# A two-layer hybrid decoder step in float32: sums of weights by adding DMAs, and modulation units spread over the blocks

## The chip, the core and the metric

The kernel runs on one core of a Trainium2 chip. Its time is the device time of one execution in microseconds. Before the change it is 3188.43 us, the median of three runs (3184.79 to 3195.4).

TensorE multiplies, VectorE and ScalarE work on vectors, GpSimd adds and multiplies and issues DMAs of its own queue, SyncE issues the loads. The profile calls them PE (PEld for its loads of weights), DVE, ACT, POOL and SP. Each takes its instructions in the order in which they were written and waits on semaphores for the others.

## The reference, cut to what matters

```python
for l in range(2):
    ada = silu(c) @ w_ada + b_ada                      # 9 vectors: shift, scale, gate of three parts
    h = rms(x) * g_ffn1 * (1 + sc1) + sh1
    x = x + 0.5 * gt1 * ((silu(h @ w1_a) * (h @ w3_a)) @ w2_a)
    h = rms(x) * g_mix * (1 + sc2) + sh2
    x = x + gt2 * mixer(h)                             # retention, conv module, short conv
    h = rms(x) * g_ffn2 * (1 + sc3) + sh3
    x = x + 0.5 * gt3 * ((silu(h @ w1_b) * (h @ w3_b)) @ w2_b)
y = rms(x) * g_final
```

There are 512 prompt positions and 8 sequences of 8 sample positions, 576 tokens in all. The model width is 1024, the SwiGLU width is 2816, everything is float32.

## The kernel before, in words

Activations lie transposed, 128 features by 576 tokens, in two halves of 288 tokens. Each float32 factor is split into a high part, which is a copy rounded to `float32r`, and a low part, which is what the rounding lost. A product is three matmuls: high by high, high by low, low by high. The high part of a weight tile is made by ScalarE (`nc.scalar.copy`, L195 and L209), the low part by VectorE (the subtraction of `rest`, L131).

**The SwiGLUs.** There are four: a and b of layer 0, then a and b of layer 1. Each has 22 column tiles `f` of `w1` and `w3`. From f = 4 on, two tiles f and f + 1 are taken together in a *seven-product block* (`seven`, L544): with quarters of `h` and of the two weight tiles, seven products of 128x512 by 512x288 give what eight would. The sums of `h` that this needs are made once (`forms`). The sums of weights are made for each block (`sums`, L213). If `a` is the raw tile of f and `b` that of f + 1, and 1 and 2 are their halves, the block needs X = a, Y with b1 + a1 in the first half of b, S = b1 + b2, and Z = a with S added to its first half and that sum of first halves to its second. GpSimd makes S, Y and Z with four additions of 128x512, in place in the raw tiles and in the buffer `s1`, of which there is one. X, S, Y and Z are each split into high and low (`halves`).

TensorE's products in a block come in the order X0, Y0, X1, Z0, S, Y1, Z1, twelve matmuls each. The first three are copied or combined on ScalarE and VectorE in between: X0's product is copied to `s1` of that function (L572), `u` is that copy plus Y0's product (L576), and Z0 adds to the bank from which `u` was made, so it waits for L576. X1 adds to the bank that L572 reads.

A SwiGLU has 18 blocks, for `w1` and `w3` by turns, in four runs of 2, 6, 4 and 6. After each run come eight *down steps*, products with `w2` over the tiles so far (the last run ends the SwiGLU).

**What sets the order.** Every engine's program is written out in the order of the Python calls. `pump` (L138), called between products, issues the loads that come next, as long as fewer than four raw tiles are held, and takes at most one *job* a call from the list that `sums` made: X's split, the additions for Z, then the splits of S, Y and Z. There are five buffers of high and low parts, so S waits until X is free, Y for S, and Z for Y. With the splits of Y and Z a raw tile each is given back, and `pump` issues the load into it (L166); SP, in its turn, waits until the old contents have been read.

**Modulation.** The vectors `ada` are a product of 9 columns with `w_ada`, cut into units (`ada_unit`, L339) of two tiles of 128x512, loaded by SP (L135) and multiplied in eight small matmuls (L349). All units run in layer 0: 56 fill its first SwiGLU and 72 its second, two after each block or pair of tiles and one after each down step, two after each down step where there are 72. Of their tiles, fewer than four are loaded ahead once the first SwiGLU is under way, and a tile counts as free three calls of `pump` after its unit.

Of the kernel before, what the change touches and what calls it, by code (L numbers as in the profile page):

```python
# [24 lines left out]
ALU = mybir.AluOpType  # L25
# [44 lines left out]
class Trunk:  # L70
# [142 lines left out]
    def sums(self, key, a, b):  # L213

        add = self.nc.gpsimd.tensor_add
        s = self.wp.tile([128, 512], F32, tag="s1", bufs=1, name=self.name("s1"))
        add(s, b[:, :512], b[:, 512:])
        add(b[:, :512], b[:, :512], a[:, :512])  # L220

        def z():
            self.rest()
            add(a[:, :512], a[:, :512], s)
            add(a[:, 512:], a[:, 512:], a[:, :512])

        def zh():
            self.halves((*key, "Z"), a)
            self.held -= 1

        def yh():
            self.halves((*key, "Y"), b)
            self.held -= 1

        self.jobs.extend(((1, lambda: self.halves((*key, "X"), a)), (0, z),
                          (1, lambda: self.halves((*key, "S"), s, 512)), (1, yh), (1, zh)))

    def part(self, key, which):
# [8 lines left out]
    def free(self, key):  # L247
        if key[0] == "ada":
            if self.quota > 8:
                self.gone.append(self.calls + 3)  # L250
            else:
                self.whole -= 1
        elif key not in self.spare:
            self.live -= 1
        del self.split[key]
# [285 lines left out]
            self.nc.vector.tensor_sub(lo, z[:, HB:], hi.bitcast(F32))  # L541
        self.zs = None

    def seven(self, key, post):  # L544

        nc = self.nc
        mm = nc.tensor.matmul
        h = [(x[0][:, :NT], x[1]) for x in self.h]
        quarter = lambda k, j: [(x[0][:, j * HB:(j + 1) * HB], x[1][:, j * HB:(j + 1) * HB]) for x in h[4 * k:4 * k + 4]]

        def product(ps, which, at, xs, first, last):
            hi, lo = self.part(key, which)
            for i, x in enumerate(xs):
                c = slice(512 * at + 128 * i, 512 * at + 128 * i + 128)
                k = dict(skip_group_check=True)
                mm(ps, hi[:, c], x[0], start=first and i == 0, stop=False, **k)  # L556
                mm(ps, hi[:, c], x[1], start=False, stop=False, **k)  # L557
                mm(ps, lo[:, c], x[0], start=False, stop=last and i == 3, **k)  # L558

        bank = lambda: self.lin(HB)  # L560
        free = lambda which: self.free((*key, which))
        def more():
            self.rest()
            for fn in self.after:
                fn()
            self.after = []
            self.pump(True)

        p, q = bank(), bank()
        product(p, "X", 0, quarter(0, 0), True, True)  # L570
        s1 = self.temp([128, HB])
        nc.scalar.copy(s1, p)  # L572
        more()
        product(q, "Y", 0, self.T[7], True, True)
        u, v = self.temp([128, HB]), s1
        nc.vector.tensor_add(u, s1, q)  # L576
        more()
        product(p, "X", 1, quarter(1, 0), False, True)
        free("X")
        post(0, 0, p)  # L580
        more()
        self.ada_done()
        product(q, "Z", 0, self.T[2], False, True)
        nc.vector.tensor_sub(v, s1, q)
        nc.vector.tensor_sub(u, u, q)
        more()
        r = bank()
        product(r, "S", 0, self.T[5], True, True)
        free("S")
        post(1, 1, v, r)  # L590
        more()
        t = bank()
        product(t, "Y", 1, self.T[4], True, True)
        free("Y")
        post(1, 0, v, t)
        more()
        product(r, "Z", 1, quarter(1, 1), False, True)
        free("Z")
        post(0, 1, u, r)
        self.rest()  # L600
        self.pump(True, False)
# [175 lines left out]
    def ffn(self, l, ab, sh, fill, first, last):  # L777

        w1, w3, w2 = "w1" + ab, "w3" + ab, "w2" + ab
        fill = deque(fill)  # L780
# [13 lines left out]
        def add_fill(n):  # L794
            for _ in range(min(n, len(fill))):
                u = fill.popleft()
                self.steps.append(([("ada", *u, i) for i in range(2)], lambda u=u: self.ada_unit(*u)))

        pairs = [[(w1, l, f), (w3, l, f)] for f in range(FT)]
# [30 lines left out]
        def one_pair(f):  # L830
            if f == 1:
                forms = self.forms()
                go(forms, 2)
                self.bg.append(forms)
            pair_step(pairs[f])

        acts = {}

        def duo_step(f, up):
            nc = self.nc  # L840
            if up == 0:
                for i in range(2):
                    g[f + i] = (self.slot([128, NT], F32R, "ghi"), self.slot([128, NT], F32R, "glo"))

            def up1(i, j, a, b=None):
                t = self.temp([128, HB])
                if b is None:
                    nc.scalar.activation(t, a, AF.Silu)
                else:
                    if i == 0:  # L850
                        nc.vector.tensor_add(t, a, b)
                    else:
                        nc.vector.scalar_tensor_tensor(t, a, -1.0, b, ALU.mult, ALU.subtract)
                    nc.scalar.activation(t, t, AF.Silu)
                acts[i, j] = t

            def up3(i, j, a, b=None):
                s = acts.pop((i, j))
                if b is None:
                    nc.vector.tensor_mul(s, s, a)  # L860
                else:
                    t = self.temp([128, HB])
                    if i == 0:
                        nc.vector.tensor_add(t, a, b)
                    else:
                        nc.vector.scalar_tensor_tensor(t, a, -1.0, b, ALU.mult, ALU.subtract)
                    nc.gpsimd.tensor_mul(s, s, t)  # L867
                c = slice(j * HB, (j + 1) * HB)
                hi, lo = (x[:, c] for x in g[f + i])

                def halves():
                    nc.scalar.copy(hi, s)
                    nc.vector.tensor_sub(lo, s, hi.bitcast(F32))  # L873

                waiting.append(halves)

            waiting = []

            def late(i, j, a, b=None):
                before = list(waiting)  # L880
                waiting.clear()
                up3(i, j, a, b)
                for fn in before:
                    fn()

            self.seven(pairs[f][up], late if up else up1)
            self.after += waiting
            if f + 2 in [at for at, _ in GROUPS] + [FT]:
                for fn in self.after:
                    fn()  # L890
                self.after = []
            if up and f + 2 == FT:
                self.T = None
# [18 lines left out]
        nfill = len(fill)  # L912
        for gi, (f0, n) in enumerate(GROUPS):
            for f in range(f0, f0 + n):
                if f == 0:
                    ks = [("ada", 0, 1, k, i) for k in range(8) for i in range(2)]
                    ks = [("do", "more_x")] + pairs[0] + ks if first else pairs[0] + pairs[1]
                    self.steps.append((ks, opening))
                elif f > 3:
                    for up in range(2 - f % 2 * 2):  # L920
                        ks = [pairs[f][up], pairs[f + 1][up]]
                        self.steps.append((ks, lambda f=f, up=up: duo_step(f, up)))
                        add_fill(2)
                elif first or f > 1:
                    self.steps.append((pairs[f], lambda f=f: one_pair(f)))
                    add_fill(2)
            final = gi == len(GROUPS) - 1
            if final:
                self.steps.append(([], self.new_norm))
            for m in range(4 if final else 8):  # L930
                k = (w2, l, m, gi)
                self.steps.append(([k], lambda k=k, final=final: down([k], final)))
                add_fill(2 if nfill > 60 else 1)
            if final:
                assert not fill
                ks = [(w2, l, m, gi) for m in range(4, 8)]
                self.steps.append((ks, lambda: down(ks, True)))
# [743 lines left out]
```

## Time and profile before

| | |
|---|---|
| median of the runs | 3188.43 us |
| profiled execution: time, span | 3193.01 us, 3191.2 us |
| PE busy | 3038.2 us, 95% |
| DVE, ACT, POOL busy | 2032.3, 1038.3, 986.4 us |
| POOL's four additions of the weight sums | 125.8, 114.8, 99.9, 96.1 us, 72 of each |
| DMA, all queues | 349.70 MB, mean 110 GB/s |
| granted clock, mean | 0.983 |

Matmuls overlap, so a matmul's own duration (some 0.3 us) is more than its share of TensorE's time. The distance between the starts of two of them is what counts: 0.13 us where TensorE doesn't wait.

### The profile page before, as it was taken

To read this page: it belongs to the slowest core of one execution; us is meant where nothing else is said; L and a number is where in the kernel's file an instruction comes from. 1 tells how busy PE (TensorE), PEld (TensorE's weight loads), DVE (VectorE), ACT (ScalarE), POOL (GpSimd) and SP (SyncE) were. 2 spreads that over 40 slices of the span, in tenths; PEclk is the share of its full clock that TensorE was granted. 3 is DMA by queue.
4 is the path that set the end of the run, shared out by engine and by line. 5 is a ranking of instruction groups with operands and counts; after the bars stand their busy time and mean duration, and the time that the engine had idled before them with its cause. 6 is when DMAs were issued, how large, how long until landed. Compare 5 with 4: busy or idle time off the path is not lost.

```text
span 3191.2 us, 55709 instructions
## 1 busy us (share of the span) xinstructions
PE 3038.2 (95%) x22548; PEld 2881.9 (90%) x22548; DVE 2032.3 (64%) x3561; ACT 1038.3 (33%) x1761; POOL 986.4 (31%) x969
## 2 busy tenths in 40 slices
PE   7999999999999998989998999999999999989998
PEld 5888898899998997878797999988999999989998
DVE  6564576355995466455577666754569954667676
ACT  3332243222232333222243333432222333333332
POOL 3152344123112022323333344442231220325452
PEclk9999999999999999999999999999999999999999
DMA  7444533335322323454431222333342223122232
GB/s 254 140 146 154 167 105 126 107 85 121 87 73 73 113 86 116 169 179 162 156 100 44 92 95 83 103 132 104 86 109 86 80 76 110 61 79 76 77 100 70
DMA packets 147298, 349.70 MB, mean 110 GB/s; under 512 B 32912, under 2 KB 37264, under 8 KB 147040
## 3 DMA queue, kind: packets, MB, share of 16 engines
q1 hardware_dynamic: 140384, 329.35, 32.3%
q0 software_dynamic: 5504, 15.61, 1.9%
q8 instruction: 177, 2.90, 0.4%
q10 hardware_dynamic: 1152, 1.18, 0.1%
q14 instruction: 81, 0.66, 0.1%
HBM read 328.90 MB, written 12.45 MB: 107 GB/s over the span
## 4 chain that ended last, share of the span: by engine, by line
PE 47%; DVE 7%; issue 2%; POOL 2%; DMA 1%; ACT 1%; SPq 0%; DVEq 0%; POOLq 0%; ACTq 0%
PE pl L284 9%; PE pl L285 9%; PE pl L286 9%; PE pl L556 5%; PE pl L558 5%; PE pl L557 5%; DVE lo L131 2%; DMA ada<-in_ada 1%; PE pm L349 1%; DVE glo L873 1%; PE pl L1025 0%; PE pl L1027 0%; PE pl L1026 0%; POOL t L867 0%; PE pm L1424 0%
## 5 line engine op out<-in xcount | busy, mean ns | idle before, releaser
L131 DVE TENSOR_TENSOR lo<-raw,hi 128x1024 fp32r<-128x1024 f32 (+2 forms) x553 | 732.6, 1330 | 241.8 <-ACT hi L195 212.1
L284 PE MATMUL pl<-hh,hi 128*128 128x288 f32 x2320 | 696.4, 300 | 29.1 <-ACT t L790 28.8
L285 PE MATMUL pl<-hl,hi 128*128 128x288 f32 x2320 | 689.2, 297 | 9.1 <-POOL hl L493 6.4
L286 PE MATMUL pl<-hh,lo 128*128 128x288 f32 x2320 | 688.1, 297 | 2.2 <-DVE lo L131 2.2
L195 ACT CAST hi<-raw 128x1024 fp32r<-128x1024 f32 (+2 forms) x337 | 315.5, 945 | 590.5 <-PE pl L285 411.9
L284 PEld LDWEIGHTS pl<-hh,hi 128*128 128x128 f32 x2320 | 439.8, 190 | 39.0 <-ACT t L790 32.1
L285 PEld LDWEIGHTS pl<-hl,hi 128*128 128x128 f32 x2320 | 440.0, 190 | 12.3 <-POOL hl L493 7.7
L286 PEld LDWEIGHTS pl<-hh,lo 128*128 128x128 f32 x2320 | 439.7, 190 | 2.9 <-DVE lo L131 2.9
L284 PE MATMUL pl<-ghi,hi 128*128 128x288 f32 x1408 | 425.4, 302 | 0.0
L285 PE MATMUL pl<-glo,hi 128*128 128x288 f32 x1408 | 418.7, 297 | 0.2
L286 PE MATMUL pl<-ghi,lo 128*128 128x288 f32 x1408 | 417.9, 297 | 0.0
L556 PE MATMUL pl<-hh,hi 128*128 128x288 f32 x1152 | 342.6, 297 | 6.6 <-ACT t L572 6.6
L558 PE MATMUL pl<-hh,lo 128*128 128x288 f32 x1152 | 340.0, 295 | 0.0
L557 PE MATMUL pl<-hl,hi 128*128 128x288 f32 x1152 | 339.6, 295 | 0.0
L209 ACT CAST hi<-raw 128x1024 fp32r<-128x1024 f32 x216 | 225.0, 1043 | 239.9 <-PE pl L285 194.1
L284 PEld LDWEIGHTS pl<-ghi,hi 128*128 128x128 f32 x1408 | 267.7, 190 | 21.4 <-issue 20.1
L285 PEld LDWEIGHTS pl<-glo,hi 128*128 128x128 f32 x1408 | 267.9, 190 | 1.1 <-DVE glo L873 1.1
L286 PEld LDWEIGHTS pl<-ghi,lo 128*128 128x128 f32 x1408 | 267.6, 190 | 0.0
L769 POOL TENSOR_TENSOR xs<-xs,t 128x64 f32<-128x64 f32 x144 | 64.2, 446 | 632.0 <-DVE t L766 621.0
L556 PEld LDWEIGHTS pl<-hh,hi 128*128 128x128 f32 x1152 | 216.4, 188 | 18.2 <-issue 7.8
L284 PE MATMUL pl<-s,hi 128*128 128x288 f32 x768 | 229.1, 298 | 0.0
L285 PE MATMUL pl<-s,hi 128*128 128x288 f32 x768 | 227.6, 296 | 1.1 <-DVE s L300 1.1
(247 smaller groups left out, 6105.3 us busy)
## 6 DMA issues: line engine op xcount, KB each, us to landing
ada<-in_ada SPq DMA_DIRECT2D x288, 256.0 KB, 4.9
raw<-in_win SPq DMA_DIRECT2D x120, 512.0 KB, 3.6
raw<-in_w1a SPq DMA_DIRECT2D x44, 512.0 KB, 3.8
raw<-in_w3a SPq DMA_DIRECT2D x44, 512.0 KB, 3.7
raw<-in_w1b SPq DMA_DIRECT2D x44, 512.0 KB, 3.7
raw<-in_w3b SPq DMA_DIRECT2D x44, 512.0 KB, 3.6
raw<-in_w2a SPq DMA_DIRECT2D x48, 384.0 KB, 3.1
raw<-in_w2b SPq DMA_DIRECT2D x48, 384.0 KB, 3.1
```

Of the source, the lines that this page charges most:

```text
L131: self.nc.vector.tensor_sub(lo, t, hi.bitcast(F32))
L195: nc.scalar.copy(hi[:, :m], t[:, c])
L209: self.nc.scalar.copy(w[0][:, :n], t[:, :n])
L284: mm(ps[:, :HB], hi[:, c], x[0][:, t], start=first, stop=False)
L285: mm(ps[:, :HB], hi[:, c], x[1][:, t], start=False, stop=False)
L286: mm(ps[:, :HB], lo[:, c], x[0][:, t], start=False, stop=last)
L349: nc.tensor.matmul(self.ps_ada[32 * j:32 * j + 32, :], self.cs[:, k], w, start=(k == 0), stop=(k == 7))
L556: mm(ps, hi[:, c], x[0], start=first and i == 0, stop=False, **k)
L557: mm(ps, hi[:, c], x[1], start=False, stop=False, **k)
L558: mm(ps, lo[:, c], x[0], start=False, stop=last and i == 3, **k)
L769: nc.gpsimd.tensor_add(xs, xs, t[:].rearrange("p b t -> p (b t)"))
L873: nc.vector.tensor_sub(lo, s, hi.bitcast(F32))
```

## The change

Three things change.

1. The sums of weights are made by DMAs that GpSimd issues and that add their source to their target. The S buffer is first loaded with b1 from memory by SP, a second time, since b1 itself becomes Y's half. Then b1 += a1, S += b2, and after X's split a2 += a1, a1 += S, a2 += S. An empty job stands between the additions for Z and the split of S.
2. Two modulation units are put into each block, between X1 and Z0, and one after it. A down step has one in all SwiGLUs.
3. A modulation tile counts as free after one call of `pump` in place of three.

```diff
-        add = self.nc.gpsimd.tensor_add
+        def add(out, x):
+            self.nc.gpsimd.dma_start(out, x, accum_op=ALU.add)
+
         s = self.wp.tile([128, 512], F32, tag="s1", bufs=1, name=self.name("s1"))
-        add(s, b[:, :512], b[:, 512:])
-        add(b[:, :512], b[:, :512], a[:, :512])
+        self.nc.sync.dma_start(s, self.source(self.duo[key])[0][:, :512])
+        add(b[:, :512], a[:, :512])
+        add(s, b[:, 512:])
 
         def z():
             self.rest()
-            add(a[:, :512], a[:, :512], s)
-            add(a[:, 512:], a[:, 512:], a[:, :512])
+            add(a[:, 512:], a[:, :512])
+            add(a[:, :512], s)
+            add(a[:, 512:], s)
...
-        self.jobs.extend(((1, lambda: self.halves((*key, "X"), a)), (0, z),
+        self.jobs.extend(((1, lambda: self.halves((*key, "X"), a)), (0, z), (0, lambda: None),
                           (1, lambda: self.halves((*key, "S"), s, 512)), (1, yh), (1, zh)))
...
-                self.gone.append(self.calls + 3)
+                self.gone.append(self.calls + 1)
...
-    def seven(self, key, post):
+    def seven(self, key, post, mids=()):
...
         self.ada_done()
+        for m in mids:
+            self.ada_unit(*m)
         product(q, "Z", 0, self.T[2], False, True)
...
-                        self.steps.append((ks, lambda f=f, up=up: duo_step(f, up)))
-                        add_fill(2)
+                        mids = [fill.popleft() for _ in range(min(2, len(fill)))]
+                        ks += [("ada", *u, i) for u in mids for i in range(2)]
+                        self.steps.append((ks, lambda f=f, up=up, mids=mids: duo_step(f, up, mids)))
+                        add_fill(2 if nfill > 72 else 1)
...
-                add_fill(2 if nfill > 60 else 1)
+                add_fill(1)
```

In the changed kernel the numbers of lines are 4 to 6 higher: L572 is L576, L867 is L873, L349 is L353. The loads of S are L221, the adding DMAs L218.

The first place is SyncE's program in a run of six blocks in layer 1, of before: pairs of raw tiles for one block after the other.

```order
L166 DMA raw3062_19223<-in_w3a 128x1024
L166 DMA raw3067_19245<-in_w3a 128x1024
L166 DMA raw3082_19354<-in_w1a 128x1024
L166 DMA raw3087_19378<-in_w1a 128x1024
L166 DMA raw3107_19494<-in_w3a 128x1024
L166 DMA raw3112_19516<-in_w3a 128x1024
```

The same place of SyncE's program now; `s1` with its number is the S buffer (s13069 is the buffer `s1`, number 3069).

```order
L166 DMA raw3062_19303<-in_w3a 128x1024
L166 DMA raw3067_19325<-in_w3a 128x1024
L221 DMA s13069_19343<-in_w1a 128x512
L166 DMA raw3082_19436<-in_w1a 128x1024
L166 DMA raw3087_19460<-in_w1a 128x1024
L221 DMA s13089_19480<-in_w3a 128x512
```

Behind each pair stands a load of the S buffer for the block of the pair before: s13089 is for the block of raw3062 and raw3067. The tile raw3087 takes the buffer of raw3034, in which Z of the block before that one was made.

The second place is ScalarE's program of the same run now, where the block of raw3034 ends its preparation and runs.

```order
L209 CAST hi3085_19457<-raw3034_19113 128x1024
L878 CAST ghi3049_19217<-t3064_19318 128x288
L576 COPY t3096_19502<-pl3094_19488 128x288
L878 CAST ghi3047_19215<-t3068_19339 128x288
L209 CAST hi3097_19506<-raw3062_19303 128x1024
L854 ACTIVATE t3100_19539<-pl3094_19488 128x288
L209 CAST hi3101_19555<-s13089_19480 128x512
```

The first row is the copy of Z of that block, the third the copy of its X0 product (pl3094), the fifth and the seventh the copies of X and S of the next block. GpSimd's program of the same run now:

```order
L218 DMA raw3034_19113<-s13069_19343 128x512 x2
L873 TENSOR_TENSOR t3059_19297<-t3059_19297,t3079_19427 128x288
L873 TENSOR_TENSOR t3064_19318<-t3064_19318,t3084_19451 128x288
L873 TENSOR_TENSOR t3068_19339<-t3068_19339,t3088_19474 128x288
L218 DMA raw3067_19325<-raw3062_19303 128x512
L218 DMA s13089_19480<-raw3067_19325 128x512
L218 DMA raw3062_19303<-raw3062_19303 128x512
L218 DMA raw3062_19303<-s13089_19480 128x512 x2
```

Five DMAs stand for a block where four additions stood, and Z of the next block takes in s13089.

The third place is in layer 0's second SwiGLU: SyncE's program now, around the S load of one block. In the block in which these loads are issued, the two units before Z0 use ada2236 and ada2237, and ada2260 and ada2261.

```order
L135 DMA ada2236_14273<-in_ada 128x512
L135 DMA ada2237_14275<-in_ada 128x512
L166 DMA raw2242_14298<-in_w1b 128x1024
L166 DMA raw2247_14322<-in_w1b 128x1024
L221 DMA s12249_14342<-in_w3b 128x512
L135 DMA ada2260_14381<-in_ada 128x512
L135 DMA ada2261_14383<-in_ada 128x512
```

The tiles of the second unit are loaded behind the pair of raw tiles and the S buffer.

## Rows read from the trace of the kernel before

**Rows 1.** The page, part 1: busy time, share of the span and instructions.
```profile
PE 3038.2 (95%) x22548; PEld 2881.9 (90%) x22548; DVE 2032.3 (64%) x3561; ACT 1038.3 (33%) x1761; POOL 986.4 (31%) x969
```

**Rows 2.** Waits of PE: engine, line, waited for: us, times, longest.
```profile
PE pm L349 <- DMA ada<-in_ada: 39.1, 24, 8.0
...
PE pl L556 <- DVE t L576: 20.3, 20, 1.8
```

**Rows 3.** Windows of down steps: us, PE busy (matmuls), clock, DMA share, GB/s.
```profile
129.10:180.60 51.50, 48.64 (x371) 0.93 0.51 176
...
sum 139.80, PE 130.50; mean PE 43.50
...
1264.10:1327.80 63.70, 55.01 (x436) 0.97 0.62 209
...
sum 174.30, PE 152.18; mean PE 50.73
...
1876.10:1914.00 37.90, 37.90 (x288) 1.00 0.29 93
1959.90:1985.80 25.90, 25.80 (x193) 1.00 0.38 122
```

**Rows 4.** The same windows, L349 alone (PE, PEld).
```profile
129.10:180.60 51.50, 7.27 (x80) 1.65 (x72) 0.93 0.51 176
...
1264.10:1327.80 63.70, 14.17 (x144) 4.07 (x136) 0.97 0.62 209
...
1519.70:1566.20 46.50, 11.49 (x112) 3.27 (x109) 0.89 0.60 204
```

**Rows 5.** Timeline of PE, two units: start, us, instructions.
```profile
1339.36 1.07 PE L349 MATMUL pm<-ada,cs 128*32 128x256 f32 x16
```

**Rows 6.** Windows of two blocks in layer 1, from X0 to the next X0.
```profile
1841.32:1852.45 11.13, 11.13 (x86) 1.00 0.29 94
1852.45:1864.68 12.23, 11.40 (x87) 1.00 0.23 66
```

**Rows 7.** Timelines of DVE and POOL ahead of the second block's Z0.
```profile
1854.52 1.82 DVE L131 TENSOR_TENSOR lo<-raw,hi 128x1024 fp32r<-128x1024 f32 x1
...
1855.22 2.27 POOL L219 TENSOR_TENSOR s<-raw 128x512 f32<-128x512 f32 x1
```

**Rows 8.** Timelines where Z is split: ACT, DVE, PE (the next X0), ACT.
```profile
1864.13 1.03 ACT L209 CAST hi<-raw 128x1024 fp32r<-128x1024 f32 x1
...
1865.34 1.22 DVE L131 TENSOR_TENSOR lo<-raw,hi 128x1024 fp32r<-128x1024 f32 x1
...
1864.68 0.29 PE L556 MATMUL pl<-hh,hi 128*128 128x288 f32 x1
...
1866.59 0.39 ACT L572 COPY t<-pl 128x288 f32<-128x288 f32 x1
```

**Rows 9.** SP in layer 0: a 512 KB and two 256 KB loads; the latter's landing.
```profile
1312.50 0.33 SPq L166 DMA_DIRECT2D raw<-in_w1b  x1
1312.92 1.18 SPq L135 DMA_DIRECT2D ada<-in_ada  x2
...
DMA to landing us min/median/max: 4.0/4.0/4.0
```

**Rows 10.** DMAs issued by POOL, and copies inside SBUF: durations (ns), KB, landing.
```profile
L1503 POOL DMA_DIRECT2D out_rets<-s0t x16: 539/549/582, 639.1 to 2345.4; - x16
...
DMA to landing us min/median/max: 2.3/2.9/10.8
...
xd<-x POOLq DMA_DIRECT2D x16, 256.0 KB, 5.1
...
x<-xd POOLq DMA_DIRECT2D x16, 256.0 KB, 4.4
...
q<-s SPq DMA_DIRECT2D x32, 72.0 KB, 2.0
```

More of the change, by code (lines that the diff above doesn't have):

```diff
@@ L837, in ffn, with duo_step @@
         acts = {}
-        def duo_step(f, up):
+        def duo_step(f, up, mids):
             nc = self.nc
@@ L884, in late @@
                     fn()
-            self.seven(pairs[f][up], late if up else up1)
+            self.seven(pairs[f][up], late if up else up1, mids)
             self.after += waiting
```

## The prediction

> **What bounds the kernel now.** I read the busy line first: TensorE is busy 95% of the span [rows 1], so only its idle time can be won, and any new wait of its own is lost in full. I then read TensorE's waits, longest first: 39.1 us for modulation blocks (24 times) and 20.3 us for the VectorE addition that frees the bank for Z0 (20 times) [rows 2]. Next come the stretches of eight (or four) down steps that stand between the runs of seven-product blocks, taken by window. Without modulation units such stretches take 37.9, 37.9 and 25.8 us, every matmul behind the last [rows 3]. With them the three stretches of layer 0's first SwiGLU take 139.8 us, and the three of its second 174.3 us. Their units number 10, 10, 10 and 18, 18, 14 (eight matmul records are a unit) [rows 4], and a unit costs TensorE 0.54 us (16 records in 1.07) [rows 5]. So the first three should take 101.6 + 30 x 0.54 = 118 us and the second 101.6 + 50 x 0.54 = 129 us: 22 and 45 us are lost there, 67 us together, half-clock time behind the stalls included (the granted clock of the stretches shown is 0.93 and 0.97).
>
> The blocks themselves run tight. One takes 11.13 us, 84 matmuls in a row; every second one takes 12.2 us [rows 6], and the whole difference is the wait before Z0. It comes from VectorE: a 128x1024 subtraction takes 1.22 us alone [rows 8] but 1.82 us while GpSimd adds a 128x512 tile (2.27 us) [rows 7].
>
> **The change, part by part.**
>
> *GpSimd's adds go.* There are 72 blocks with four adds each. None is on TensorE's path by itself, but VectorE loses its slow neighbour, and in layer 0 two modulation units stand ahead of Z0 and cover the same wait. I count all 20.3 us of that wait as won. If VectorE is late for another reason, up to 20 us of that stay.
>
> *Modulation units are spread.* The second SwiGLU's down stretches get one unit a step where they had two; a freed tile counts as free two pump calls earlier. They become at most as bad as the first SwiGLU's stretches are (22 us in three), at best free of loss. The gain is between 45 - 22 = 23 and 67 us; I take 45, the middle. The units themselves cost the same wherever they stand.
>
> *The adding DMAs form a loop that had no DMA in it.* The rows of SP's order show it: the load of the next block's S buffer stands behind the load into the buffer of this block's Z, and that one waits until this block's Z has been split. From the end of Z's subtraction in one block to the same point in the next, every hop waits for the hop before:
> SP issues the 512 KB load and 0.42 us later the 256 KB one, which lands 4.0 us after its issue: 4.4 us [rows 9]. S += b lands after A. The add inside `a` was issued 0.55 us behind it and lands that much later. Then the two adds of S into `a` go out, 0.55 us apart, and the second lands after A. ScalarE copies 1.03 us, VectorE subtracts 1.22 us [rows 8]. Four hand-overs cost about 0.1 us each (an estimate: between the last two it was 0.18). The sum is R = 4.4 + A + 0.55 + 0.55 + A + 1.03 + 1.22 + 0.4 = 8.2 + 2A.
> In the kernel before, GpSimd's adds needed only loads that had been issued a block earlier, so TensorE set the pace.
>
> *A, the landing of a 256 KB adding DMA,* isn't in the trace. From below: plain copies of 72 KB inside SBUF, issued by SP, land after 2.0 us. From above: the 256 KB copies that GpSimd issues in bursts land after 4.4 and 5.1 us, say 4.7. Nearest are the 16 that it issues one or two at a time: 2.3 at least, 2.9 in the median [rows 10]. An adding DMA reads its target too, so I don't go below that median: A = 2.9, R = 14.0.
> The Trainium skill ("DMA: Bandwidth & Descriptors", Anatomy of one DMA) gives a GpSimd-issued DMA 2.0 us plus its bytes at 436 GB/s, most of it the receipt of the last byte, which every dependent DMA pays again: a rule against chains of small DMAs. By it A would be an estimated 2.6, R 13.4 and the time about 3196 us; the rows' 2.3 to 2.9 agree with it for plain copies.
>
> *Layer 1* (two SwiGLUs, runs of 2, 6, 4 and 6 blocks). A run's first two blocks are prepared during the down steps. In block 1 Z's copy ends 0.5 us after X0 starts (1865.16 against 1864.68) [rows 8]. The copy of X0's product stands behind Z's copy on ScalarE (the order rows show that too), with a 0.43 us operation between, and X1 needs it at X0 + 3.2: so Z's copy may end at X0 + 2.3 and the slack is 1.8 us. From there each block adds R - 11.1 = 2.9 us. A run of six loses 4 x 2.9 - 1.8 = 9.8, one of four 2 x 2.9 - 1.8 = 4.0, one of two nothing. A SwiGLU loses 23.6 us, two lose 47.
>
> *Layer 0.* A block with its three units takes 11.1 + 1.6 = 12.7 us. Here the second unit inside the block uses two tiles whose loads stand on SP behind the same pair of loads. They land about 0.85 us after S, 5.25 us after Z's subtraction; then come the unit (0.54), Z0, S and Y1 (4.75), and Z's split, which ended 3.46 us after Z1 began [rows 8]: a loop of 14.0 us, the same as R. The subtraction ended 1.9 us after the next X0, so 1.3 us with a unit between; 1.3 + 5.25 is 1.25 us past the place of that unit (X0 + 5.3). A run of six loses 1.25 + 4 x 1.3 = 6.5, of four 3.9, of two 1.25, and the last run, nearly out of units, 9.8 as in layer 1: 21.4 a SwiGLU, 43 for two.
>
> **Sum.** +47 + 43 - 45 - 20 = +25 us. The profiled execution took 3193.0 us (span 3191.2 and 1.8 around it), so 3218; it is 4.6 us above the median of the runs, so I forecast 3213 us. Within this case (A from 2.6, half way down to the least landing, to 3.4, half a microsecond above the median; growth 2.3 to 3.9 us a block) it is 3196 to 3253.
>
> **Rivals.**
> *The chain is short: faster.* Source and target are both in SBUF, and the 72 KB copies there took 2.0 us. At A = 2.0, R is 12.2: layer 1 loses 2 x (2 x 2.6 + 0.4) = 11, layer 0, held by its modulation loads, 2 x (1.25 + 6.5 + 3.9 + 2.6) = 28. Against gains of 65 to 87 that is -26 to -48 us: about 3150 us. It decides where losses fall below gains, near A = 2.5. Against it: no 256 KB DMA of GpSimd's landed in less than 2.3 us, and these read twice.
> *The queue is crowded: far slower.* Five 256 KB adds and an extra load per block come on top of weights, at a DMA share that is 0.6 already in layer 0's stretches [rows 3]. At A = 4.7, R is 17.6: 119 us in layer 1 and 2 x (1.25 + 20.9 + 11 + 24.2) = 115 in layer 0, less 65: 3357 us. The Trainium skill ("SBUF — State Buffer", the sections on the two sides and on bandwidth pools) says that VectorE's two-port operations keep GpSimd from writing descriptors, so that a DMA of 620 ns took 3100; 2.5 us more on each A would put the time, by estimate, past 3400 us. What the trace shows for it is only the wide spread of landings, 2.3 to 10.8 us [rows 10].
> *Nothing moves.* Losses and gains cancel within 10 us, most likely with A near 2.5 to 2.6: 3188 us.
>
> **How the numbers follow.** I give the forecast's case 0.50, the short chain 0.28, the crowded queue 0.14 and no change 0.08. 0.3% (10 us) is about what a measurement of this kernel can tell from none. Faster takes the short chain and a sliver of the rest, 0.29; same 0.11; slower 0.60. For the range, 3140 holds most of the short chain and 3320 most of the crowded queue.
>
> **What would show it.** If I am right: blocks late in a run start some 14 us apart in layer 1, with ScalarE's copy of X0's product as TensorE's releaser ahead of X1; SP's S load comes right behind a load that waited for VectorE; TensorE's wait for modulation tiles shrinks in the down steps and reappears inside layer 0's blocks; the wait before Z0 in its old form is gone; GpSimd is busy far less, but waits. If blocks of layer 1 keep 11.1 us to the end of a run, the loop doesn't bind and the forecast is wrong; if the adds land after 4 us or more, its size is.

## The result, and the profile after

The changed kernel takes 3546.14 us (median of four runs, 3543.31 to 3551.2) against 3189.97 us before: ratio 1.1118, 95% interval 1.1094 to 1.1142. The forecast was 3213 us, with a range of 3140 to 3320. The sign was right and the size was not: 356 us lost where 25 were expected.

The page of the changed kernel begins with the busy line that answers to [rows 1].

```profile
PE 3171.5 (89%) x22548; PEld 2972.5 (84%) x22548; DVE 1899.3 (54%) x3561; ACT 1028.9 (29%) x1761; POOL 847.9 (24%) x1041
```

VectorE is relieved by 133 us, as its slow neighbour is gone, and the share of TensorE falls to 89%. Its waits, in the form of [rows 2]:

```profile
PE pl L560 <- ACT t L576: 135.0, 44, 7.6
PE pm L353 <- DMA ada<-in_ada: 74.6, 48, 4.9
PE pl L562 <- DVE lo L131: 56.4, 26, 4.3
...
PE pl L560 <- DVE t L580: 0.6, 1, 0.6
```

The wait ahead of Z0 for the freed bank (L580 now) is gone, as forecast. In its place stand the wait ahead of X1 for ScalarE's copy of X0's product (L576), the wait ahead of Y0 for Y's low part (L562), and twice the wait for modulation tiles. The first is the sign that the prediction named for its loop. The second it did not name: Y's split stands behind that of S, which waits for the add into S.

Windows of the down steps of layer 0's second SwiGLU, then of its first, against [rows 3]:

```profile
1364.92:1412.63 47.71, 46.06 (x364) 40.17 (x363) 21.05 (x41) 8.36 (x11) 8.47 (x15) 1.00 0.75 209
...
sum 131.97, PE 125.67 PEld 107.99 DVE 57.81 ACT 23.54 POOL 26.69; mean PE 41.89 PEld 36.00 DVE 19.27 ACT 7.85 POOL 8.90
...
sum 120.50, PE 117.87 PEld 106.16 DVE 54.27 ACT 22.25 POOL 27.71; mean PE 39.29 PEld 35.39 DVE 18.09 ACT 7.42 POOL 9.24
```

Cut in the same way, from the last block's end to the next one's start, they took 175.2 and 140.8 us before. They are 64 us shorter now; 35 of their units, 19 us by 0.54 each, have moved into the blocks. That leaves the 45 us that were forecast, at full clock (1.00).

The loss is in the blocks. The runs of layer 1's first SwiGLU (2, 6, 4, 6 blocks; the last run and the sum), after and then before:

```profile
2207.10:2317.74 110.64, 81.73 (x507) 79.39 (x506) 45.01 (x75) 31.04 (x52) 27.35 (x33) 0.83 0.58 132
sum 308.35, PE 235.34 PEld 228.58 DVE 131.77 ACT 90.92 POOL 76.21; mean PE 58.84 PEld 57.14 DVE 32.94 ACT 22.73 POOL 19.05
```

```profile
1985.76:2054.72 68.96, 67.33 (x507) 66.86 (x505) 52.97 (x75) 31.22 (x51) 36.94 (x28) 1.00 0.29 89
sum 208.56, PE 201.95 PEld 200.55 DVE 153.53 ACT 93.79 POOL 94.50; mean PE 50.49 PEld 50.14 DVE 38.38 ACT 23.45 POOL 23.63
```

So 100 us go in this SwiGLU, and 99 in the next. In layer 0 the blocks grow by 117 and 119 us, 19 of them the units that moved in, so 217 us are lost there. Losses of 199 and 217, less the 45 won and 13 won outside these stretches, make 358 us, by which the spans differ.

One lap of the loop, from the end of VectorE's subtraction for Z of one block (layer 1, 3208.42) to the same point a block later (3226.69). SyncE, GpSimd, ScalarE and VectorE, each from its timeline:

```profile
3208.45 0.33 SPq L166 DMA_DIRECT2D raw<-in_w3b  x1
3208.82 0.43 SPq L221 DMA_DIRECT2D s<-in_w1b  x1
```

```profile
3213.05 0.85 POOL L218 DMA_DIRECT2D s<-raw  x1 [11.51 <-DMA s<-in_w1b]
3213.58 1.19 POOL L218 DMA_DIRECT2D raw<-raw  x1
3218.75 1.73 POOL L218 DMA_DIRECT2D raw<-s  x2 [3.98 <-issue]
```

```profile
3223.69 1.05 ACT L209 CAST hi<-raw 128x1024 fp32r<-128x1024 f32 x1 [1.93 <-DMA raw<-s]
```

```profile
3225.47 1.22 DVE L131 TENSOR_TENSOR lo<-raw,hi 128x1024 fp32r<-128x1024 f32 x1
```

The landings in this lap: of the S load, of the first two rows of GpSimd (the second lands last), and of its two adds of S (likewise):

```profile
DMA to landing us min/median/max: 3.7/3.7/3.7
...
DMA to landing us min/median/max: 3.9/4.3/4.6
...
DMA to landing us min/median/max: 3.3/3.8/4.3
```

S is asked for 0.40 us after the subtraction ends and lands 3.67 later. GpSimd's add into S goes out 0.56 after that, the add inside `a` 0.53 behind it, and this one lands after 4.65. After 0.52 the two adds of S go out, 0.53 apart, and the second lands after 4.30. ScalarE starts 0.11 later and takes 1.05; VectorE, whose order has another operation first, starts 0.73 later and takes 1.22. That is 0.40 + 3.67 + 0.56 + 0.53 + 4.65 + 0.52 + 0.53 + 4.30 + 0.11 + 1.05 + 0.73 + 1.22 = 18.27 us, the whole lap: every hop is one that the prediction listed. In the lap before, the next block's add for Y goes out right behind the adds of S, and a raw tile is loaded then. The landing row is of the two adds of S at 3198.94 and 3199.48 and that add, at 3200.01 (least, median, longest):

```profile
3198.94 1.72 POOL L218 DMA_DIRECT2D raw<-s  x2 [3.66 <-DMA raw<-raw]
3200.01 1.52 POOL L218 DMA_DIRECT2D raw<-raw  x1
...
DMA to landing us min/median/max: 3.6/6.5/7.3
```

The second add of S, the middle one, lands after 6.5 us there in place of 4.3. So it goes in all 14 blocks of layer 1 that are fourth or later in their run: the second add of S lands after 4.3 us where nothing goes out beside it (4 blocks), after 5.2 to 7.1 beside the load of a raw tile (6, each the last of its run), and after 6.5 to 8.0 where the add for Y goes out as well (4).

### The profile page after: what moved, and what is told of

It reads as the page before. It is cut to its first block, busy times and chain, and to the rows that moved or that the text cites. A ratio compares the mean times of both kernels' runs of the same rounds, so it can differ in the third digit from the quotient of the medians.

```text
span 3549.4 us, 56464 instructions
## 1 busy us (share of the span) xinstructions
PE 3171.5 (89%) x22548; PEld 2972.5 (84%) x22548; DVE 1899.3 (54%) x3561; ACT 1028.9 (29%) x1761; POOL 847.9 (24%) x1041
## 3 DMA queue, kind: packets, MB, share of 16 engines
q0 software_dynamic: 57344, 110.00, 17.6%
## 5 line engine op out<-in xcount | busy, mean ns | idle before, releaser
L131 DVE TENSOR_TENSOR lo<-raw,hi 128x1024 fp32r<-128x1024 f32 (+2 forms) x553 | 661.3, 1203 | 451.6 <-ACT hi L209 232.6
L288 PE MATMUL pl<-hh,hi 128*128 128x288 f32 x2320 | 695.5, 300 | 18.7 <-ACT t L796 18.4
L289 PE MATMUL pl<-hl,hi 128*128 128x288 f32 x2320 | 688.7, 297 | 9.1 <-POOL hl L497 6.4
L290 PE MATMUL pl<-hh,lo 128*128 128x288 f32 x2320 | 687.8, 296 | 2.2 <-DVE lo L131 2.2
L560 PE MATMUL pl<-hh,hi 128*128 128x288 f32 x1152 | 377.1, 327 | 161.2 <-ACT t L576 135.0
L288 PEld LDWEIGHTS pl<-hh,hi 128*128 128x128 f32 x2320 | 439.3, 189 | 27.7 <-ACT t L796 20.5
L289 PEld LDWEIGHTS pl<-hl,hi 128*128 128x128 f32 x2320 | 439.4, 189 | 12.3 <-POOL hl L497 7.7
L290 PEld LDWEIGHTS pl<-hh,lo 128*128 128x128 f32 x2320 | 439.1, 189 | 2.9 <-DVE lo L131 2.9
L562 PE MATMUL pl<-hh,lo 128*128 128x288 f32 x1152 | 369.4, 321 | 56.5 <-DVE lo L131 56.4
L560 PEld LDWEIGHTS pl<-hh,hi 128*128 128x128 f32 x1152 | 240.6, 209 | 188.9 <-ACT t L576 145.2
L561 PE MATMUL pl<-hl,hi 128*128 128x288 f32 x1152 | 364.8, 317 | 0.0
L562 PEld LDWEIGHTS pl<-hh,lo 128*128 128x128 f32 x1152 | 241.9, 210 | 62.8 <-DVE lo L131 62.8
L561 PEld LDWEIGHTS pl<-hl,hi 128*128 128x128 f32 x1152 | 241.4, 210 | 0.0
L288 PE MATMUL pl<-s,hi 128*128 128x288 f32 x768 | 229.5, 299 | 0.0
```

What stands on the lines that cost most here:

```text
L131: self.nc.vector.tensor_sub(lo, t, hi.bitcast(F32))
L288: mm(ps[:, :HB], hi[:, c], x[0][:, t], start=first, stop=False)
L289: mm(ps[:, :HB], hi[:, c], x[1][:, t], start=False, stop=False)
L290: mm(ps[:, :HB], lo[:, c], x[0][:, t], start=False, stop=last)
```

## The experiments

In the expectations, "growth of a block" is what a block takes beyond the 11.1 us of its matmuls.

**Either part alone.** First the changed kernel with GpSimd's additions back and without the empty job.

```diff
-        def add(out, x):
-            self.nc.gpsimd.dma_start(out, x, accum_op=ALU.add)
+        add = self.nc.gpsimd.tensor_add
...
```

> The changed kernel with GpSimd's four additions back and without the empty job: modulation units spread, a tile free after one call, nothing else. Theory (the loss is the loop of adding DMAs; the spread is a gain): the down steps keep what they show in the changed kernel, 45 us less than before at equal units, and the wait ahead of Z0 goes in layer 0: 3190 - 45 - 10 = 3135 us. Rival (units inside the blocks are themselves late: TensorE's wait for modulation tiles is 74.6 us in the changed kernel, most of it inside blocks): most of that stays, about 3190 - 45 + 60 = 3205 us.

3207.81 us, ratio 1.0056 (1.0039 to 1.0072): near the rival. The spread alone is a loss. The down steps gain what they gained in the changed kernel (119.6 and 128.3 us), layer 1 is as before, and layer 0's blocks take 81 us more, 62 beyond the units moved. SyncE and TensorE in one of these blocks (X0 at 1342.25, Z0 at 1350.37):

```profile
1342.32 1.83 SPq L166 DMA_DIRECT2D raw<-in_w3b  x2
1344.24 2.92 SPq L135 DMA_DIRECT2D ada<-in_ada  x6
```

```profile
1347.22 0.64 PE L349 MATMUL pm<-ada,cs 128*32 128x256 f32 x8
1349.09 1.35 PE L349 MATMUL pm<-ada,cs 128*32 128x256 f32 x8 [1.23 <-DMA ada<-in_ada]
```

The first unit runs at once. The second needs the first two of six tiles that are loaded behind the block's raw tiles and land 4.8 to 5.0 us after their issue.

Then the adding DMAs without the spread (the three edits on units undone):

```diff
-                add_fill(1)
+                add_fill(2 if nfill > 60 else 1)
...
```

> The kernel before with the adding DMAs, the second load of S and the empty job, units as before. Theory (the adds carry the whole loss and layer 0's blocks wait for them as layer 1's do): the changed kernel without its gain in the down steps, 3546 + 45 = about 3590 us. Rival (the units inside the blocks cause layer 0's part, 217 us of the loss): layer 1 loses its 199 us, layer 0 little: about 3390 us.

3535.13 us, 1.1085 (1.1062 to 1.1107). The adds carry the loss, though it is 55 us less than the theory's figure. Layer 1's blocks lose 100 us a SwiGLU (308.4 and 310.4 us), layer 0's 73 and 74, less than in the changed kernel.

**What the chain is made of.** The same DMAs as copies, which leave the sums out:

```diff
-            self.nc.gpsimd.dma_start(out, x, accum_op=ALU.add)
+            self.nc.gpsimd.dma_start(out, x)
```

> The changed kernel with the five DMAs as plain copies, without adding, so the sums are left out; same places, sizes and waits. Theory (a DMA that adds takes longer than one that copies, since it reads its target too; the price of 2.9 us was taken from copies): the landings fall, the add into S from 3.3 to about 2.6 us, the one behind it from 4.3 to about 3.3, the adds of S likewise, so a lap falls from 19 to about 17 us and the time to about 3450 us. Rival (adding costs nothing; the landing is that of two DMAs in a row on GpSimd's queue): landings and time unchanged, 3546 us within 20.

3308.79 us (one run), 237 us less than the changed kernel: the theory's direction, and more than its size. The pages' rows of DMA issues (KB each, median us to landing), changed kernel and then plain copies:

```profile
raw<-raw POOLq DMA_DIRECT2D x144, 256.0 KB, 4.6
raw<-s POOLq DMA_DIRECT2D x144, 256.0 KB, 4.3
...
s<-raw POOLq DMA_DIRECT2D x72, 256.0 KB, 3.4
```

```profile
raw<-raw POOLq DMA_DIRECT2D x144, 256.0 KB, 2.9
raw<-s POOLq DMA_DIRECT2D x144, 256.0 KB, 2.6
s<-raw POOLq DMA_DIRECT2D x72, 256.0 KB, 2.5
```

And the rows of GpSimd's queue (packets, MB, time of its packets as a share of 16 engines' span) of the changed kernel, of plain copies and of before:

```profile
q0 software_dynamic: 57344, 110.00, 17.6%
```

```profile
q0 software_dynamic: 34304, 110.00, 9.4%
```

```profile
q0 software_dynamic: 5504, 15.61, 1.9%
```

For the same bytes the adding DMAs hold each of the 16 DMA engines (17.6% of 3549 us less 1.9% of 3191) / 360 = 1.57 us each, the copies (9.4% of 3307 less 61) / 360 = 0.69.

The changed kernel without the add inside `a`, which leaves out a part of Z's sum:

```diff
-            add(a[:, 512:], a[:, :512])
```

> The changed kernel without the add of a's first half to its second, so that part of Z's sum is left out; four adding DMAs a block. Theory (of two adding DMAs issued 0.54 us apart the second lands 1.5 us after the first, and the adds of S wait for it): the chain now waits for the add into S alone, 1.5 us a lap less, laps of about 17.5 us: some 1.5 us in each of 48 growing blocks plus shorter half-clock time, about 3460 us. Rival (the adds of S, not these, carry the chain, or the blocks wait for something else): within 25 of 3546 us.

3418.54 us (one run): the theory, and 40 us further.

The S load moved ahead of the raw tiles:

```diff
         def yh():
+            self.rest()
+            nxt = self.keys[self.raw[0][0]] if self.raw else None
+            if nxt in self.duo:
+                self.early[nxt] = self.load_s(nxt)
...
```

> The changed kernel with one thing moved: SyncE issues the load of the next block's S buffer as soon as S of this block is split, ahead of the two raw tiles, so it no longer waits for Z's split. Same DMAs, same bytes. Theory (what counts is the chain of waits): the chain from Z's split to the next Z's split loses the wait for the S load (about 5 us of 19); what binds next is ScalarE's copy of X behind Z's copy, VectorE's subtraction, the add inside a, the adds of S, Z's copy: 1.0 + 0.5 + 1.2 + 0.6 + 4.3 + 0.6 + 0.5 + 4.3 + 1.1 = 14.1 us. Growth of a block falls from 8 to 3 us, the loss in the blocks from 416 to about 160 to 200 us: about 3310 us. Rival (GpSimd's queue or the DMA engines can't move five adds and 1.25 MB of loads in a block, whatever they wait for): same DMAs, so no change, 3546 us within 25.

3405.12 us, 1.0677 (1.0656 to 1.0698). With the same DMAs 141 us are won, so what GpSimd's queue can move is not what set the pace; but 95 us of the theory's gain are missing. SyncE in one block of layer 1 shows why:

```profile
3306.35 0.33 SPq L216 DMA_DIRECT2D s<-in_w1b  x1
3306.79 2.31 SPq L167 DMA_DIRECT2D raw<-in_w3b  x2
```

The S load goes out when the second add of S has landed (3306.29), since that add reads the one buffer. The expectation had S free after its split. The chain then lost only the copy and the subtraction of Z and the raw load's issue.

S made by GpSimd:

```diff
-        self.nc.sync.dma_start(s, self.source(self.duo[key])[0][:, :512])
+        self.nc.gpsimd.tensor_add(s, b[:, :512], b[:, 512:])
...
-        add(s, b[:, 512:])
```

> The changed kernel with S made by one addition on GpSimd (b1 + b2, as before the change) in place of the second load and the add into it; four adding DMAs a block are left. Theory (chain of waits): the same chain of 14.1 us as with the S load moved ahead, so about 3310 us, within 30 of that kernel. Rival (capacity): one DMA in five and one load in three fewer, so the blocks' growth falls by a fifth to a third: 3410 to 3460 us.

3384.13 us, 1.0611 (1.0590 to 1.0632): 21 us from the kernel with the S load first, as the theory said, but with it 74 us above the theory's figure, and 26 below the rival's range. This run alone decides little.

Over all of these, from each trace the mean over layer 1's 14 blocks that are fourth or later in their run (from the X1 of the block before to its own, and the mean landings of the add into S, the one inside `a`, the second add of S):

| kernel | block | into S | inside a | second of S | time |
|---|---|---|---|---|---|
| before | 11.9 | | | | 3190 |
| changed | 19.6 | 3.4 | 4.4 | 5.8 | 3546 |
| plain copies | 14.8 | 2.3 | 2.6 | 2.7 | 3309 |
| no add inside a | 17.0 | 3.3 | | 4.6 | 3419 |
| S first | 16.5 | 4.9 | 5.1 | 5.1 | 3405 |
| S by GpSimd | 16.4 | | 3.7 | 5.7 | 3384 |

The block follows the sum of its chain's landings and hops: copies take 1.8 + 3.1 = 4.9 us out of two landings in a row, and the block is 4.8 us shorter. The second of these landings no longer depends on what goes out beside it: in the 14 blocks it takes 2.6 to 2.7 us, once 4.2.

**The empty job.**

```diff
-        self.jobs.extend(((1, lambda: self.halves((*key, "X"), a)), (0, z), (0, lambda: None),
+        self.jobs.extend(((1, lambda: self.halves((*key, "X"), a)), (0, z),
```

> The changed kernel without the empty job, so S's split is asked for one pump call earlier. Theory (chain from Z to Z sets the pace and S's split is not in it): within 20 of 3546 us. Rival (ScalarE then takes S's copy earlier in its order and waits there for the add into S, which holds the copies of X0's product behind it): 3570 to 3620 us.

3521.84 us, 1.1041 (1.1011 to 1.1071): some 24 us better than with it, neither what the theory nor what the rival said. In its trace the second add of S lands after 4.9 us in the mean of the 14 blocks, and a block takes 18.9 us, 0.7 less. It is a small part of the loss, and why the adds land sooner was not followed further.

**The units' place and the tiles held.** Spread only, the two units 4.8 us later in the block:

```diff
+        for m in mids:
+            self.ada_unit(*m)
         product(r, "Z", 1, quarter(1, 1), False, True)
...
```

> Spread only (GpSimd's additions, no adding DMA), with the two units of a block moved from ahead of Z0 to ahead of Z1, 4.8 us later in the block. Theory (the units' tiles are loaded behind the block's two raw tiles and land 7 to 11 us after X0 starts, so units at X0 + 5 wait and units at X0 + 9.6 hardly do): nearly all of the 62 us lost in layer 0's blocks by the spread goes, the wait ahead of Z0 comes back there (10 us): 3208 - 62 + 10 = about 3155 us. Rival (the loads for three units and two raw tiles are too much for a block of 12.7 us, so the same time is lost a little later): 3190 to 3208 us.

3360.09 us, 1.0538 (1.0517 to 1.0558): both wrong by far. The first row of TensorE's waits:

```profile
PE pm L349 <- DMA ada<-in_ada: 164.8, 32, 8.0
```

With units ahead of Z1 their tiles are held to the block's end. The third unit's tiles, for which there is no room among four, then stand behind the next block's raw loads, and TensorE waits for them behind Z1 in 25 of layer 0's 36 blocks, 6.1 us in the mean. So it is not the distance from X0 that counts but how many tiles may be held. Hence the spread with six:

```diff
-RAW, WB, AHEAD, ADA, ADA_LATER = 4, 5, 4, 12, 4
+RAW, WB, AHEAD, ADA, ADA_LATER = 4, 5, 4, 12, 6
```

> Spread only (GpSimd's additions, units ahead of Z0 as in the change), with fewer than six modulation tiles loaded ahead in place of fewer than four. Theory (three units a block need six tiles; with four, the second unit's two tiles can only be loaded behind the raw tiles of its own block): with six they come with the block before, TensorE's wait inside blocks goes and the down steps keep their gain: 3190 - 45 - 10 = about 3135 us. Rival (the transfers themselves, 1.5 MB of modulation and 1 MB of weights in a block, are late): still above 3185 us.

3149.58 us, 0.9863 (0.9848 to 0.9878), faster than both kernels. TensorE's waits:

```profile
PE pl L284 <- ACT t L792: 30.0, 12, 5.7
PE pl L556 <- DVE t L576: 16.3, 18, 1.1
...
PE pm L349 <- DMA ada<-in_ada: 9.0, 3, 7.8
```

The wait for tiles is 9.0 us where before had 39.1 [rows 2]. The bytes are the same as in the spread alone, so it was not their amount that made the tiles late. Of the 15 us missing to the theory's figure, some are the wait ahead of Z0, which hardly shrinks. Six tiles in the kernel before, by the same line:

> The kernel before with fewer than six modulation tiles loaded ahead and nothing else. Theory (in the down steps of before the units wait since two a step use up four tiles faster than they land): two tiles more shorten part of the 67 us lost there, 3150 to 3175 us. Rival (the down steps are held by the bytes, 0.6 of the DMA engines' time): within 10 of 3190 us.

3166.80 us, 0.9919 (0.9902 to 0.9936), as the theory had it: six tiles give 28 us by themselves, and the spread 17 more with them.

The spread with six tiles (the edit is against it) and one adding DMA a block, off the chain:

```diff
-        add(b[:, :512], b[:, :512], a[:, :512])
+        self.nc.gpsimd.dma_start(b[:, :512], a[:, :512], accum_op=ALU.add)
```

> The spread with six tiles ahead, and one of the four additions, b1 + a1 for Y, made by an adding DMA, which nothing on the chain from Z to Z waits for; S and Z stay on GpSimd. Theory (an adding DMA costs only where a chain waits for its landing; Y is needed about two products after S): within 8 us of the spread with six tiles, or up to 8 better as GpSimd slows VectorE less ahead of Z0. Rival (any adding DMA in the block holds ScalarE's order up, as the changed kernel's did): 30 us and more above it.

3148.89 us, 0.9865 (0.9847 to 0.9883): no difference in time from the one without it. Something does wait for it, though: the trace has a row that the spread with six tiles lacks, again ahead of Y0.

```profile
PE pl L558 <- DVE lo L131: 5.1, 5, 1.9
```

Layer 1's blocks take 9 us longer (425.2 against 416.1 us), and as much is won in other places. So an adding DMA off the chain costs nothing in the whole here; that it is free at its place is not shown.

The changed kernel with six tiles:

> The changed kernel whole, with fewer than six modulation tiles loaded ahead in place of fewer than four. Theory (the spread and the adding DMAs cost apart from each other, as 16 and 340 us of the profiled executions add up to the changed kernel's 358): six tiles give back what they gave the spread alone, 58 us: about 3490 us. Rival (in layer 0's blocks the chain of adding DMAs covers the wait for tiles): within 20 of 3546 us.

3544.88 us, 1.1105 (1.1056 to 1.1154): the rival. TensorE's waits:

```profile
PE pl L560 <- ACT t L576: 153.8, 51, 7.7
...
PE pl L560 <- DVE t L859: 36.1, 16, 4.6
PE pm L353 <- DMA ada<-in_ada: 21.1, 9, 8.0
```

The wait for tiles falls from 74.6 to 21.1 us and comes back as waits for the chain; layer 0's blocks keep their 340 us (348 and 339). That 16 and 340 us add up to the changed kernel's 358 is therefore no proof that the two parts cost side by side.

## Why the prediction was wrong

*What bounds the kernel, and the gains: right in the main.* The down steps gave their 45 us; as 45 was the middle of a range of 23 to 67, hitting it is luck in part. The wait ahead of Z0 went, but that it went with GpSimd's additions is not shown: the new waits ahead of Y0 and X1 come before it in the same block. The prediction's sentence "the units themselves cost the same wherever they stand" failed. With four tiles held, three units in a block cost 62 us more than where they had stood, which the spread alone shows and the spread with six tiles nearly takes away. The prediction had seen that the second unit's tiles stand behind the raw loads. It put their lateness down to a loop through the S load, which the spread alone does not have.

*The loop: right, with one wait overlooked.* Order of hops, the wait ahead of X1, the S load behind a load that waited for VectorE, blocks that grow late in a run: all is in the trace, and hops taken out shorten the block. What the prediction lacks is the wait ahead of Y0 for Y's split (56.4 us for its low part). One of its signs failed: GpSimd was to be busy far less, and is busy 848 us in place of 986, as issuing one adding DMA keeps it busy for 0.85 to 1.19 us in the rows shown.

*Its size: the step that failed is "A, the landing of a 256 KB adding DMA", and with it the hand-overs.* A = 2.9 was the landing of copies, and the upper bound of 4.7 was that of copies in a burst. For copies it holds: with plain copies they land after 2.3 to 2.7 us and a block takes 14.8 us, where R was 14.0. By the Trainium skill ("DMA: Bandwidth & Descriptors", Anatomy of one DMA) A would be an estimated 2.6 us; the copies agree, the adds don't. An add lands in the mean after 3.4 us when it goes out first and 4.4 behind another; the second add of S after 5.8, which mixes 4.3 with nothing beside it and 5.2 to 8.0 with other transfers. The prediction's own sign that the size is wrong, adds that land after 4 us or more, is what happened. In the sum of R the two landings are 4.4 + 5.8 in place of 2.9 + 2.9, and each of GpSimd's two answers to a landing takes 0.52 to 0.56 us where 0.1 was estimated: 14.0 + 4.4 + 0.9 = 19.3, and 19.6 is measured. The prediction said that an adding DMA "reads its target too" and used this only to rule out less than the median, where it should have moved the value up.

With 19.6 the prediction's formula (growth 8.5; four growing blocks in a run of six, two in one of four, 1.8 off each) gives 159 us for layer 1 in place of 47; 199 were lost. Of the other 40 us, 8 are in the runs of two, which lost 3 to 5 us where none was expected. 11 stand behind the last X1 of the six longer runs, where TensorE no longer waits but part of the time has the lower of its two clocks behind the longer waits (granted clock 0.77 to 0.84, 59.4 us in all; before 1.00, 48.7 us). And the growth starts a block earlier than the prediction had it: between the first two X1 of these runs stood 12.1 to 17.8 us, 11.1 before. For layer 0 the prediction's formula with 19.6 gives 2 x (1.25 + 4 x 6.9 + 1.25 + 2 x 6.9 + 1.25 + 32.2) = 155 us in place of 43; 217 were lost. So this step makes up 112 + 112 = 224 us of the 331 by which the forecast missed.

*The rivals.* The crowded queue had the size nearest (R of 17.6, 3357 us), with the reason half right: an add is slower by itself, and slower again with others behind it. That all transfers together were too many is refuted by the S load moved ahead. The reason that the Trainium skill gives in that rival, VectorE's two-port operations ("SBUF — State Buffer", the section on bandwidth pools), did not show where it could be told apart: plain copies at the same places in layer 1's first SwiGLU landed after 2.6 us in the median and 4.4 at most. Over the whole kernel they took up to 7.4 us, and no run separates that reason from the other transfers there.

*Open:* why layer 0's blocks lose 217 us in the changed kernel and 147 with the adds alone, although waits for tiles are covered by the chain. In its late blocks the add into S lands after 4.7 us against 3.7 there, and six modulation tiles go out with them in place of four; no run separates the two.

## What to carry to other kernels

Before an operation on an engine is turned into a DMA, write down who waits for its landing: off the chain one a block changed nothing in the whole time, and on it each hop cost its landing and another half microsecond. A price taken from a simpler operation is a lower bound, and the range has to say so. Where consumers of prefetched tiles are moved closer together, count the tiles that may be held at once before anything else.

## What the runs showed of the hardware

An adding DMA of 256 KB inside SBUF holds its engines 1.57 us where a copy holds them 0.69, and lands 1.1 us later when it goes out first (3.4 against 2.3, means of the 14 blocks). Of two issued 0.5 us apart the second add lands some 1.5 us after the first, the second copy 0.8. With the load of a raw tile, or that and a third add, beside them, the second add of S landed after 5.2 to 8.0 us in place of 4.3; copies at these places after 2.6 to 2.7, once 4.2. Between the landing that GpSimd waits for and the start of its next DMA stood 0.52 to 0.56 us in the lap shown.
